# The recorder's reckoning of transfers set to longer landings, and one gate tile's room given to the common pool

## The chip, the cores and the metric

The kernel runs on one core of a Trainium2 chip. The metric is the device time of one execution in microseconds (us), lower being better. Three runs of the kernel before took 814.87, 815.20 and 815.69 us; the median is 815.20 us.

## The reference, cut to what matters

It computes one step of a one-layer decoder for 512 prompt tokens and 8 samples of 4 tokens, 544 columns in all, which share every weight:

```python
h = rmsnorm(x, norm_mix); z = h @ w_in             # attention and HGRN2 heads
x = x + concat([att, o]) @ w_out                   # 1024 wide
x = x + (cross-attention to 256 memory rows) @ w_co
u = rmsnorm(x, norm_ffn)
ug = u @ w_gate                                    # 1024 -> 2816
conv = conv_b + sum(conv_w[j] * up[:, j:j + T] for j in range(3))  # up: ug behind two kept rows
x = x + (silu(conv) * (u @ w_up)) @ w_down         # 2816 -> 1024
```

Everything is float32. The last two gate rows of each sequence are an output too.

## The kernel before, in words

Activations lie transposed, features on the 128 partitions and the 544 tokens along the row. Each float32 operand of a product is split in two rounded parts, a high one (h) and a low one (l): ScalarE (ACT) rounds the high part with a cast, VectorE (DVE) subtracts it to get the low one. A product is then three TensorE (PE) passes: high by high, high by low, low by high.

The feed-forward stage has 22 gate tiles g0 to g21 and 22 up tiles u0 to u21. The first six are computed plainly; the others in pairs by a scheme of seven half-size products in place of eight (class `Pair`, L2315). A pair's weights come in as one tile of 512 KB (wrg or wru, which holds A11 and A12), one of 256 KB (A22) and two sums S1 and S3. A sum is a 256 KB load on SyncE's queue (SP) followed by a second, adding transfer that GpSimd (POOL) issues into the same tile (`load_sum`, L2045). DVE makes S2 and S4 from S1. Each of the seven matrices is then split by a cast on ACT and a subtraction on DVE (`split_a`, L2076). On PE a pair's seven products run in the order 1, 2, 6, 7, 5, and its products 3 and 4 among those of the next pair. Products 1, 6, 5 and 3 add up in one bank of PE's memory, ps_a (ps_ag or ps_au by kind). Between them ACT copies that bank out: after product 1 into ps_d, after product 6 and after product 5 into a tile called kept (L2381). PE can't go on in that bank until the copy is done.

The down projection is three groups of such products on gate and up tiles 0 to 3, 4 to 7 and 8 to 11 (class `DownPair`, L2172), slipped between the pairs' products; a last part follows at the end. Its banks are ps_aw, ps_cw and ps_dw, and after its first product ACT copies ps_aw into ps_dw (L2241). A22 of two down pairs is loaded by POOL: two loads into A22w_h, a negating cast on ACT into A22w_l, and two adding loads into A22w_l (`load_split`, L2053). X, U, T and V (wX, wU and so on) are sums of tokens that DVE makes and ACT casts.

What sets the order of the work is a recorder, class `Tape`. The kernel's code doesn't issue instructions; it records steps, with the tiles that each reads and writes. PE's products of the main line keep a given order. `Tape.order` (L462) then plays all engines on a table of durations and so writes out one order per engine: at each moment an engine starts that step among the ready ones which is due first. A step may start when its due time is near (`lead`) and when its tiles' pools have room. The due times go backward from the main products (`due`, L417): a step is due its user's due time less `takes` (L263). For a transfer, `takes` and the moment at which its users become ready come from `Step.alone` (L269) and from the lines at L575 to L579: so many us fixed, so many for the bytes, alone and behind other transfers.

Each engine executes its instructions in the order so written and stops at one whose operand isn't there. SP and POOL issue transfers in that way too: an instruction whose tile is not yet free, or whose first load hasn't landed, holds up all behind it.

Two pools matter here. `A` (L736) gives tiles of 544 columns from a common pool of NA of them; weights, sums and parts come from it. `G` (feed-forward stage) gives tiles of 564 columns from a pool of NG: each gate tile ug and each convolution result cv takes one. A ug tile is free when the convolution has read it and POOL has copied its last rows into `last2` (L1991), a cv tile when the up tile has been multiplied by it.

Of the kernel before, what the change touches and what calls it, by code (L numbers as in the profile page):

```python
# [53 lines left out]

HT = N // 2
NBB = 12
NG = 5
LEVELS = (1, 2, 4, 8, 16, 32, 64)
FW = N
NA = 70  # L60


ROWS = [16 * i + j for i in range(96) for j in range(TS)] + list(range(1536, 2048))
# [189 lines left out]
class Step:  # L253
# [15 lines left out]
    def alone(self):  # L269

        if self.engine == "POOL":
            return 3.6 + 1.5 * self.bytes / 300e3 + 0.9 * (len(self.calls) - 1)
        return max(2.5 + self.bytes / 300e3, 1.1 + self.bytes / 170e3)


class Tape:
# [185 lines left out]
    def order(self):  # L462
# [22 lines left out]
        now, clock, bus, todo, done, burst, first = 0.0, [0.0, 0.0], 0.0, len(self.steps), [], False, None  # L485
# [15 lines left out]
        def held_back(s, after=0):  # L501

            block, wait = (codes + s.codes + len(hears(s)) // 2 + after - 1) // self.BLOCK, 0.0
            for b in range((codes - 1) // self.BLOCK + 1, block + 1):
                share = min(1.0, (b * self.BLOCK - codes) / s.codes)
                asked = now + max(0.0, ((b - 1) * self.BLOCK - 64 - codes) / s.codes) * s.length
                at = now + wait + share * s.length
                wait += max(0.0, fetched.get(b, asked + self.FETCH + queued()) - at)
            return wait
# [4 lines left out]
        def fetch(s, wait):  # L514
            nonlocal codes
            news = hears(s)
            codes += len(news) // 2
            heard.update(news)
            for b in range((codes - 1) // self.BLOCK + 1, (codes + s.codes - 1) // self.BLOCK + 1):
                fetched.setdefault(b + 1, now + wait + self.FETCH)  # L520
            for b in range((codes + 63) // self.BLOCK + 1, (codes + s.codes + 63) // self.BLOCK + 1):
                share = max(0.0, (b * self.BLOCK - codes - 64) / s.codes)
                fetched[b + 1] = now + share * (wait + s.length) + self.FETCH + queued()
            codes += s.codes
# [3 lines left out]
        def active(at):  # L528

            done = 0.0  # L530
            for a, b, work in reversed(ran):
                if b <= at - self.SPELL:
                    break
                done += work * (b - max(a, at - self.SPELL)) / (b - a)
            return done

        def needs(s):
            want = {}
            for n in s.tiles:
                if n in self.kinds and n not in held:  # L540
                    want[self.kinds[n]] = want.get(self.kinds[n], 0) + 1
            return want
# [22 lines left out]
        def start(s):  # L565
            nonlocal todo, bus, mode
            waiting[s.engine].remove(s)
            for k, v in needs(s).items():
                room[k] -= v
            for n in s.tiles:  # L570
                if n in last and n not in held:
                    ends[n] = last[n]
            held.update(n for n in s.tiles if n in self.kinds)
            s.start, s.nth = now, len(done)
            if s.bytes:  # L575
                pool = s.engine == "POOL"
                free[s.engine] = now + (0.9 * len(s.calls) if pool else 0.4)
                bus = max(bus, now) + (1.5 if pool else 1.0) * s.bytes / 300e3
                s.end = max(bus + (3.6 if pool else 2.5), now + s.alone())  # L579
            else:  # L580
                held_up = max(0.0, port[s.engine == "DVE"] - now) if s.port else 0.0
                if s.port:
                    port[s.engine == "POOL"] = now + held_up + s.length
                if s.engine == "PE":
                    held_up = held_back(s) + self.SWITCH * (s.mode != mode)
                    fetch(s, held_up)
                    mode = s.left_in
                    if now > 12.0 and now > cold[1] and active(now) < self.IDLE * self.SPELL:
                        cold[:] = cold[0] + self.COLD, now + 2 * self.SPELL
                    ran.append((now, now + held_up + s.length, s.work))  # L590
                free[s.engine] = s.end = now + held_up + s.length
            if s.main:
                clock[:] = s.est, now
            for n in s.tiles:
                if n in self.kinds:
                    left[n] -= 1
                    if not left[n]:
                        ends.pop(n, None)
                        frees.append((s.end + s.lag, self.kinds[n]))
            todo -= 1  # L600
            done.append(s)
            seen = set()
            for u in s.users:
                if u in seen:
                    continue
                seen.add(u)
                if s not in u.deps:
                    at = s.start
                elif u.engine == s.engine and not s.bytes:
                    at = s.start + s.length - 0.05  # L610
                else:
                    at = s.end + s.lag
                u.ready = max(u.ready, at)
                u.waits -= 1
                if not u.waits:
                    waiting[u.engine].append(u)

        while todo:
# [4 lines left out]
            for e in ("SP", "ACT", "DVE", "POOL"):  # L623
                if free[e] <= now + 1e-9:
                    at = clock[0] + min(now - clock[1], 4.0)
                    can = [s for s in waiting[e] if s.ready <= now + 1e-9 and s.begin <= at + (s.lead or self.LEAD) and fits(s)]
                    if can:
                        busy = port[e == "DVE"] > now + 0.1
                        start(min(can, key=lambda s: (s.begin + 2.0 * (s.port and busy), s.number)))
                        moved = True  # L630
            if free["PE"] <= now + 1e-9:
                can = [s for s in waiting["PE"] if s.ready <= now + 1e-9 and fits(s)]
                main = [s for s in can if s.main]
                side = [s for s in can if not s.main]
                if main:
                    side = [s for s in side if held_back(s, 96) < 0.1
                            and active(now + s.length) + s.work >= self.ACTIVE * self.SPELL]
                if side and first is None:
                    first = now
                even = [s for s in side if s.mode == s.left_in == mode == (128, 128)]  # L640
                if side and (burst or even or not main or sum(s.length for s in side) >= self.BURST
                             or now - first > self.PATIENCE
                             or min(s.begin for s in side) < clock[0] + now - clock[1]):
                    s = min(side, key=lambda s: (s.begin + self.NEAR * (s.mode != mode), s.number))
                    if not burst and even and main and sum(s.length for s in side) < self.BURST:
                        s = min(even, key=lambda s: (s.begin, s.number))
                    else:
                        burst, first = True, None
                    start(s)
                    moved = True  # L650
                elif main:
                    start(main[0])
                    burst = False
                    moved = True
            if not moved:
# [9 lines left out]
                now = min(t for t in later if t > now + 1e-9)  # L665
# [57 lines left out]
def tile_decoder_step(ctx: ExitStack, tc: tile.TileContext, xT, memT, kwT, vw, s0, conv_in, mkT, mv, vecs, cst,  # L723
# [12 lines left out]
    def A(name, shape=None, dt=F32):  # L736
        return tape.tile(act, shape or [128, FW], dt, tag="a", name=name, bufs=NA)

    def R(name):
        return tape.tile(act, [128, FW], F32R, tag="a", name=name, bufs=NA)[:, :N]  # L740

# [1199 lines left out]
    def G(name):  # L1941
        return tape.tile(ffn, [128, 564], F32, tag="g", name=name, bufs=NG)

# [847 lines left out]
```

## Time and profile before

| what | value |
| --- | --- |
| median of three runs | 815.20 us |
| the profiled execution's own time | 816.82 us |
| its span, first to last instruction | 815.0 us |
| PE busy | 795.2 us (98%) |
| DVE busy | 663.2 us (81%) |
| ACT busy | 465.7 us (57%) |
| POOL busy | 196.4 us (24%) |
| feed-forward stage | about 435 us to the end |
| granted TensorE clock | 0.997 |

The profile is one execution. Times in it are us from the span's start; the profiled run took 816.82 us, 1.8 us more than its span and 1.6 us more than the median. A row of the timeline is start, duration, engine, line, operation, output<-inputs, shapes and count, and in brackets how long the engine had been idle before it and what ended that. Buffer numbers are left out of its names: ps_dw is any down pair's ps_dw, and S3g6h is the high part of gate pair 6's S3. L718 and L690 are the lines of the recorder's wrapper, so all instructions have one of these two. SPq and POOLq rows are issues of transfers; a transfer's landing time is counted from its issue.

### The profile page before, as it was taken

To read this page: it belongs to the slowest core of one execution; us is meant where nothing else is said; L and a number is where in the kernel's file an instruction comes from. 1 tells how busy PE (TensorE), PEld (TensorE's weight loads), DVE (VectorE), ACT (ScalarE), POOL (GpSimd) and SP (SyncE) were. 2 spreads that over 40 slices of the span, in tenths; PEclk is the share of its full clock that TensorE was granted. 3 is DMA by queue.
4 is the path that set the end of the run, shared out by engine and by line. 5 is a ranking of instruction groups with operands and counts; after the bars stand their busy time and mean duration, and the time that the engine had idled before them with its cause. 6 is when DMAs were issued, how large, how long until landed. Compare 5 with 4: busy or idle time off the path is not lost.

```text
span 815.0 us, 19168 instructions
## 1 busy us (share of the span) xinstructions
PE 795.2 (98%) x7432; PEld 747.8 (92%) x7432; DVE 663.2 (81%) x1484; ACT 465.7 (57%) x996; POOL 196.4 (24%) x282
## 2 busy tenths in 40 slices
PE   9999999999999999999999998999899899999995
PEld 8998888987888889999899998999899899999995
DVE  6889786688598976654679898998999899989973
ACT  8724468616458454434466566655655666568642
POOL 1131100030120300312334144433334234141023
PEclk9999999999999999999999999999999999999998
DMA  9745996799742374362642386778678878876403
GB/s 316 238 144 148 316 288 187 261 331 304 232 140 82 108 253 136 101 191 90 183 139 58 74 209 148 170 161 209 158 170 162 194 170 173 197 185 196 102 2 110
DMA packets 106699, 143.35 MB, mean 176 GB/s; under 512 B 7280, under 2 KB 73712, under 8 KB 106608
## 3 DMA queue, kind: packets, MB, share of 16 engines
q1 hardware_dynamic: 91296, 123.77, 48.5%
q0 software_dynamic: 14592, 17.83, 14.2%
q8 instruction: 58, 0.95, 0.5%
q10 hardware_dynamic: 720, 0.53, 0.2%
q14 instruction: 33, 0.27, 0.1%
HBM read 134.04 MB, written 8.07 MB: 174 GB/s over the span
## 4 chain that ended last, share of the span: by engine, by line
PE 85%; DMA 6%; ACT 3%; DVE 3%; issue 1%; POOL 0%; SPq 0%; DVEq 0%; POOLq 0%; ACTq 0%
PE ps_wo L718 6%; PE ps_ag L718 4%; PE ps_au L718 4%; DMA S3g<-in_w_gate 4%; PE ps_aw L718 3%; PE ps_q L718 3%; PE ps_co L718 3%; PE ps_cq L718 3%; PE ps_dz L718 3%; PE ps_g L718 3%; PE ps_az L718 2%; PE ps_hv L718 2%; PE ps_first L718 2%; PE ps_cu L718 2%; PE ps_cg L718 2%; PE ps_ck L718 2%
## 5 line engine op out<-in xcount | busy, mean ns | idle before, releaser
L718 DVE TENSOR_TENSOR wl<-wr,wh 128x512 fp32r<-128x512 f32 x102 | 72.0, 729 | 1.2 <-ACT wh L718 1.2
L718 ACT CAST wh<-wr 128x512 fp32r<-128x512 f32 x102 | 58.5, 615 | 19.9 <-DMA wr<-in_w_out 7.0
L718 POOL TENSOR_TENSOR hG<-hG,hf 128x256 f32<-128x256 f32 (+1 forms) x28 | 25.0, 892 | 147.7 <-DVE hf L718 79.4
L718 POOL COPY last<-ug 128x2 f32<-128x2 f32 (+1 forms) x44 | 25.3, 618 | 94.1 <-DVE ug L718 84.0
L718 DVE SCALAR_TENSOR_TENSOR cv<-ug,vec,cv 128x560 f32<-128x560 f32 x44 | 35.1, 798 | 1.6 <-ACT cv L718 1.1
L718 POOL TENSOR_TENSOR acc_cx<-acc_cx,sq_cx 128x256 f32<-128x256 f32 (+1 forms) x14 | 11.5, 818 | 65.2 <-ACT sq_cx L718 65.2
L718 ACT ACTIVATE cv<-cv 128x560 f32<-128x560 f32 x22 | 14.8, 674 | 15.2 <-DVE cv L718 15.1
L718 ACT ACTIVATE cv<-ug,vec 128x560 f32<-128x560 f32 x22 | 18.8, 856 | 6.6 <-DVE ug L718 4.2
L718 POOL COPY ug<-conv_state 128x16 f32<-128x16 f32 x22 | 20.7, 941 | 0.0
L718 ACT ACTIVATE P<-P,mx 128x128 f32<-128x128 f32 (+3 forms) x32 | 17.6, 553 | 5.0 <-DVE mx L718 4.8
L718 DVE TENSOR_TENSOR xr<-xr,ps_wo 128x256 f32<-128x256 f32 (+1 forms) x16 | 6.9, 437 | 16.0 <-PE ps_wo L718 16.0
L690 POOL DMA_DIRECT2D S13w<-in_w_down x12 | 12.5, 1038 | 28.5 <-DVE cv L718 14.8
L718 PE MATMUL ps_co<-coh,wh 128*128 128x256 f32 (+1 forms) x64 | 19.2, 301 | 0.0
L718 PE MATMUL ps_co<-coh,wl 128*128 128x256 f32 (+1 forms) x64 | 18.4, 288 | 0.0
L718 PE MATMUL ps_co<-col,wh 128*128 128x256 f32 (+1 forms) x64 | 18.4, 287 | 0.0
L718 DVE TENSOR_TENSOR up<-ps_cu,keptu 128x272 f32<-128x272 f32 x20 | 8.7, 436 | 10.4 <-ACT keptu L718 8.0
L690 POOL DMA_DIRECT2D A22w_0l<-in_w_down x6 | 10.2, 1695 | 27.5 <-ACT S2g14h L718 10.5
L718 POOL TENSOR_TENSOR acc_ux<-acc_ux,sq_ux 128x256 f32<-128x256 f32 (+1 forms) x13 | 11.9, 916 | 17.7 <-ACT sq_ux L718 17.5
L718 POOL TENSOR_TENSOR acc_final<-acc_final,sq_final 128x256 f32<-128x256 f32 (+1 forms) x10 | 9.1, 922 | 28.4 <-ACT sq_final L718 28.4
L718 ACT COPY hsm<-psA 64x128 f32<-64x128 f32 x4 | 1.0, 259 | 26.1 <-PE psA L718 26.1
L718 DVE TENSOR_TENSOR xr<-xr,ps_aw 128x272 f32<-128x272 f32 x36 | 15.5, 430 | 0.3 <-PE ps_aw L718 0.3
L718 PE MATMUL psd<-st,qbd_win 128*32 128x224 f32 x256 | 15.6, 358 | 0.0
(3269 smaller groups left out, 3759.4 us busy)
## 6 DMA issues: line engine op xcount, KB each, us to landing
st<-in_kwT SPq DMA_DIRECT2D x32, 448.0 KB, 5.9
st<-in_vw SPq DMA_DIRECT2D x28, 512.0 KB, 6.4
wr<-in_w_in SPq DMA_DIRECT2D x25, 512.0 KB, 6.5
wru<-in_w_up SPq DMA_DIRECT2D x10, 512.0 KB, 6.9
wrg<-in_w_gate SPq DMA_DIRECT2D x9, 512.0 KB, 6.9
st<-in_mkT SPq DMA_DIRECT2D x8, 512.0 KB, 4.9
wr<-in_w_out SPq DMA_DIRECT2D x8, 512.0 KB, 4.7
S13w<-in_w_down SPq DMA_DIRECT2D x24, 128.0 KB, 3.1
```

What stands on the lines that cost most here:

```text
L690: return tape.put(engine, lambda: call(*args, **kw), outs, ins, 0.1, 0.3, size)
L718: return tape.put(engine, lambda: call(*args, **kw), outs, ins, length, lag, size, port, codes, work, mode)
```

## The change

Four lines of the recorder's table of transfers are other numbers, and two pool sizes:

```diff
-NG = 5
+NG = 4
-NA = 70
+NA = 71
...
         if self.engine == "POOL":
-            return 3.6 + 1.5 * self.bytes / 300e3 + 0.9 * (len(self.calls) - 1)
-        return max(2.5 + self.bytes / 300e3, 1.1 + self.bytes / 170e3)
+            return 5.5 + 2.0 * self.bytes / 300e3 + 0.9 * (len(self.calls) - 1)
+        return max(3.0 + self.bytes / 300e3, 1.1 + self.bytes / 90e3)
...
-                bus = max(bus, now) + (1.5 if pool else 1.0) * s.bytes / 300e3
-                s.end = max(bus + (3.6 if pool else 2.5), now + s.alone())
+                bus = max(bus, now) + (2.0 if pool else 1.0) * s.bytes / 300e3
+                s.end = max(bus + (5.5 if pool else 3.0), now + s.alone())
```

By this table a lone 256 KB transfer (262,144 bytes) of SP counted 3.4 us and now counts 4.0; one of 512 KB counted 4.2 and now 6.9; a 256 KB transfer of POOL counted 4.9 and now 7.2. No instruction of the computation is added or removed. The order in which ACT, DVE, POOL and SP have their instructions changes throughout the feed-forward stage and at many places before it. On PE the order of the main products is the same; between 95 us and 430 us the smaller products of attention, HGRN2 and cross attention stand at other places among them, and in the feed-forward stage PE's order is unchanged.

Three places, each before and after. The first is on POOL's queue, at the first down group (about 488 to 500 us of the profile). S1g6 and S3g6 are the adding transfers of gate pair 6, last2<-ug the copies of a gate tile's last rows, A22w0_0h the down group's loads. Before:

```order
L690 DMA S1g6_1464<-in_w_gate 128x512
L718 COPY last2_1250<-ug5_1413 128x2
L718 COPY last2_1250<-ug5_1413 128x16
L690 DMA S3g6_1471<-in_w_gate 128x512
L718 COPY last2_1250<-ug4_1390 128x2
L718 COPY last2_1250<-ug4_1390 128x16
L690 DMA A22w0_0h_1496<-in_w_down 128x2x128 x2
```

After:

```order
L690 DMA S1g6_1464<-in_w_gate 128x512
L690 DMA A22w0_0h_1496<-in_w_down 128x2x128
L690 DMA S3g6_1471<-in_w_gate 128x512
L690 DMA A22w0_0h_1496<-in_w_down 128x2x128
L718 COPY last2_1250<-ug5_1413 128x16
L718 COPY last2_1250<-ug5_1413 128x2
L718 COPY last2_1250<-ug4_1390 128x2
L718 COPY last2_1250<-ug4_1390 128x16
```

S3g6's transfer stood behind the copies of ug5 and now stands ahead of them, with one load of A22w0_0h ahead of it. At the second and third groups (S3g10, S3g14) the copies already stood ahead of the transfers; there both loads of A22w_0h, which stood behind S3g's transfer, now stand between S1g's and S3g's, with copies of a gate tile between the two loads.

The second place is ACT's queue at the second down group (about 567 to 575 us): casts, a convolution's start (cv9), the copy of ps_au8 into kept that PE's product 3 waits for, and the copy of ps_aw0 into ps_dw. Before, directly behind the cast of S1g10:

```order
L718 ACTIVATE cv9_1616<-ug9_1577,vec_72 128x560
L718 CAST S3g10h_1650<-S3g10_1649 128x512
L718 CAST A22u8h_1655<-A22u8_1654 128x512
L718 COPY keptu8_1605<-ps_au8_1583 128x272
L718 CAST wXh4_1487<-wX4_1481 128x272 x2
L718 CAST S24w4_0h_1640<-S24w4_0_1639 128x512
L718 CAST wUh4_1485<-wU4_1482 128x272
L718 ACTIVATE A22w4_0l_1675<-A22w4_0h_1674 128x512
L718 COPY ps_dg10_1624<-ps_ag10_1623 128x272
L718 CAST wUh4_1485<-wU4_1482 128x272
L718 CAST S2g10h_1644<-S2g10_1643 128x512
L718 COPY ps_dw0_1629<-ps_aw0_1628 128x272
```

After, from that cast on:

```order
L718 CAST S1g10h_1671<-S1g10_1642 128x512
L718 CAST A22u8h_1655<-A22u8_1654 128x512
L718 ACTIVATE A22w4_0l_1675<-A22w4_0h_1674 128x512
L718 ACTIVATE cv9_1616<-ug9_1577,vec_72 128x560
L718 COPY keptu8_1605<-ps_au8_1583 128x272
L718 CAST S24w4_0h_1640<-S24w4_0_1639 128x512
L718 CAST wUh4_1485<-wU4_1482 128x272 x2
L718 CAST S3g10h_1650<-S3g10_1649 128x512
L718 COPY ps_dg10_1624<-ps_ag10_1623 128x272
L718 CAST S2g10h_1644<-S2g10_1643 128x512
L718 COPY ps_dw0_1629<-ps_aw0_1628 128x272
```

The cast of S3g10 moved from ahead of the copy into kept to behind it. The cast of A22u8 and the negating cast A22w4_0l now both stand ahead of cv9, and the casts of wX stand behind the copy into ps_dw. At the third group (632 to 641 us) it is alike, but there the casts of wX stay ahead of the copy into ps_dw and the cast of S3g14 stands ahead of them. At the first group (502 to 509 us) the casts of A22u4, S1g6 and h4 come ahead of S3g6's, and behind it stand wX, A22w0_0l, S24w0_0, wX and the first half of wU, and only then the copy into kept; behind that, the second half of wU, cv5, S2g6, ps_dg, A11u6, and then the copy into ps_dw.

The third place is ACT's queue at about 714 us, where up pair 18 begins; ps_du18 is the copy that PE's product 2 waits for. Before:

```order
L718 CAST S4u18h_2030<-S4u18_2029 128x512
L718 CAST h17h_1991<-up17_1965 128x544
L718 COPY ps_du18_2000<-ps_au18_1999 128x272
L718 COPY ug18_1978<-ps_ag18_1969 128x240
L718 COPY ug18_1978<-ps_ag18_1969 128x8x4
L718 ACTIVATE cv18_2004<-ug18_1978,vec_72 128x560
```

After:

```order
L718 CAST S4u18h_2030<-S4u18_2029 128x512
L718 COPY ps_du18_2000<-ps_au18_1999 128x272
L718 CAST S1g20h_2051<-S1g20_2037 128x512
L718 COPY ug18_1978<-ps_ag18_1969 128x240
L718 COPY ug18_1978<-ps_ag18_1969 128x8x4
L718 ACTIVATE cv18_2004<-ug18_1978,vec_72 128x560
L718 CAST S2g20h_2039<-S2g20_2038 128x512
L718 CAST h17h_1991<-up17_1965 128x544
```

The cast of h17 moved from ahead of that copy to behind it, and one of S1g20 stands there instead.

At the last of ACT's places of which the prediction speaks (735 to 745 us, up pair 20) the casts of S4u20 and A22u20 change sides about the copy into ps_du20, and a cast into wdh and one into A11h change sides about the first copy into kept; the number of casts ahead of the second copy is the same.

On SP, in the mixing stage, some loads of weights (wr) moved behind one or more loads of cached rows (st), as wr16 behind st35; in the feed-forward stage S1g10's load moved ahead of A1w4_0's and S1g14's ahead of A1w8_0's.

## Prediction

> **What bounds the kernel now.** First the page's busy times, then the busy times by stretches of the feed-forward stage (columns: PE, weight load, DVE, ACT, POOL, clock, DMA share, GB/s).
>
> ```profile
> PE 795.2 (98%) x7432; PEld 747.8 (92%) x7432; DVE 663.2 (81%) x1484; ACT 465.7 (57%) x996; POOL 196.4 (24%) x282
> 450.00:500.00 50.00, 50.00 (x400) 50.00 (x399) 45.90 (x91) 29.48 (x56) 17.47 (x25) 1.00 0.58 144
> 50.00:310.00 260.00, 259.51 (x3034) 223.50 (x3027) 212.18 (x562) 143.20 (x322) 33.29 (x41) 1.00 0.68 213
> 571.40:637.50 66.10, 63.71 (x504) 63.27 (x504) 60.48 (x130) 39.92 (x84) 23.23 (x36) 1.00 0.79 176
> 637.50:703.00 65.50, 63.81 (x503) 63.25 (x504) 62.48 (x130) 41.58 (x86) 22.31 (x37) 1.00 0.76 171
> ```
>
> PE bounds it, at full clock. Where it never stops it issues 400 products in 50 us, 0.125 us each; 12 of them, one half-size product of a pair, take 1.5 us. What it can still gain is its stops, listed by the waits and shown one by one by the timeline:
>
> ```profile
> PE ps_dw L718 <- ACT ps_dw L718: 4.2, 3, 1.7
> PE ps_au L718 <- ACT keptu L718: 3.7, 4, 1.4
> 506.09 0.40 PE L718 MATMUL ps_au<-B22h,S4u4h 128*128 128x272 f32 x1 [1.36 <-ACT keptu L718]
> 508.68 0.39 PE L718 MATMUL ps_dw<-h1h,A1w_0h 128*128 128x272 f32 x1 [0.82 <-ACT ps_dw L718]
> 571.44 0.40 PE L718 MATMUL ps_au<-B22h,S4u8h 128*128 128x272 f32 x1 [0.60 <-ACT keptu L718]
> 574.88 0.39 PE L718 MATMUL ps_dw<-h5h,A1w_0h 128*128 128x272 f32 x1 [1.67 <-ACT ps_dw L718]
> 637.51 0.39 PE L718 MATMUL ps_au<-B22h,S4u12h 128*128 128x272 f32 x1 [0.69 <-ACT keptu L718]
> 640.96 0.39 PE L718 MATMUL ps_dw<-h9h,A1w_0h 128*128 128x272 f32 x1 [1.67 <-ACT ps_dw L718]
> 715.13 0.39 PE L718 MATMUL ps_du<-B21h,A12u18h 128*128 128x272 f32 x1 [0.50 <-ACT ps_du L718]
> 745.02 0.39 PE L718 MATMUL ps_au<-B22h,S4u20h 128*128 128x272 f32 x1 [1.04 <-ACT keptu L718]
> ```
>
> Eight stops, 8.35 us; the first product behind a stop runs 0.1 us longer (0.40 against 0.29), so they cost 9.2 us. Why ACT copies so late is in its timeline, and for the first stop in POOL's:
>
> ```profile
> 502.71 0.62 ACT L718 CAST S3g6h<-S3g 128x512 fp32r<-128x512 f32 x1 [2.42 <-DMA S3g<-in_w_gate]
> 503.24 0.42 ACT L718 CAST h4h<-up 128x272 fp32r<-128x272 f32 x1
> 503.56 0.62 ACT L718 CAST A22u4h<-A22u 128x512 fp32r<-128x512 f32 x1
> 504.92 0.85 ACT L718 ACTIVATE cv<-ug,vec 128x560 f32<-128x560 f32 x1
> 505.67 0.36 ACT L718 COPY keptu<-ps_au 128x272 f32<-128x272 f32 x1
> 567.26 0.62 ACT L718 CAST S1g10h<-S1g 128x512 fp32r<-128x512 f32 x1 [2.82 <-DMA S1g<-in_w_gate]
> 569.96 0.62 ACT L718 CAST S3g10h<-S3g 128x512 fp32r<-128x512 f32 x1 [1.32 <-DMA S3g<-in_w_gate]
> 571.01 0.38 ACT L718 COPY keptu<-ps_au 128x272 f32<-128x272 f32 x1
> 632.50 0.62 ACT L718 CAST S1g14h<-S1g 128x512 fp32r<-128x512 f32 x1 [2.35 <-DMA S1g<-in_w_gate]
> 635.29 0.62 ACT L718 CAST S3g14h<-S3g 128x512 fp32r<-128x512 f32 x1 [2.18 <-DMA S3g<-in_w_gate]
> 637.10 0.36 ACT L718 COPY keptu<-ps_au 128x272 f32<-128x272 f32 x1
> 493.77 3.81 POOL L718 COPY last<-ug 128x2 f32<-128x2 f32 x2 [4.83 <-DVE ug L718]
> 497.53 0.86 POOL L690 DMA_DIRECT2D S3g<-in_w_gate  x1
> ```
>
> ACT stands still for a sum that hasn't landed, with the copy that PE needs queued behind the cast. The old table put those casts too early: it counted 4.9 us for POOL's adding transfer, and the table of issues has more (KB each, median us to landing):
>
> ```profile
> S1g<-in_w_gate POOLq DMA_DIRECT2D x9, 256.0 KB, 6.1
> S3g<-in_w_gate POOLq DMA_DIRECT2D x9, 256.0 KB, 7.0
> S3g<-in_w_gate SPq DMA_DIRECT2D x9, 256.0 KB, 3.3
> A22w_0h<-in_w_down POOLq DMA_DIRECT2D x6, 128.0 KB, 8.4
> ```
>
> The Trainium skill ("DMA: Bandwidth & Descriptors", on the anatomy of a DMA issued by GpSimd) gives about 2.0 us plus the bytes at 436 GB/s. By that page a 256 KB transfer would take an estimated 2.6 us, the old table would already be generous, and the change would gain nothing. The rows disagree here: 7.0 us in the median, with a second transfer ahead on the same queue and a DMA share near 0.8.
>
> **The change part by part.** ACT steps follow each other at 0.32 us (a cast of 272, 503.24 to 503.56), 0.53 (a cast of 512, 502.71 to 503.24), 0.75 (cv, 504.92 to 505.67), about 0.3 (a copy).
>
> *First group.* S3g6's transfer no longer stands behind ug5's copies, which held it until 497.53. Its base was long there, so it goes behind S1g6's and one load, some 6 us sooner, and lands before ACT comes to it: the 2.42 us stand-still goes. Next late is DVE: one wU cast now stands ahead of the copy into kept.
>
> ```profile
> 502.83 0.78 DVE L718 TENSOR_TENSOR wU<-wX,up 128x272 f32<-128x272 f32 x2
> ```
>
> The first wU is ready near 503.3, so the copy runs near 503.7, in time for PE, which came to it at 504.73 (506.09 less 1.36): 1.36 saved. Behind the copy stand wU, cv5, S2g6, ps_dg and A11u6, 0.3 + 0.32 + 0.75 + 0.53 + 0.3 + 0.53 = 2.7 us, so the copy into ps_dw starts near 506.4. PE goes on 0.43 us behind a copy's start (505.67 to 506.09), at 506.8; it is there at 504.73 + 1.5 = 506.2 and waits 0.6 in place of 0.82. Saved: 1.5.
>
> *Second group.* S3g10's cast stands behind the copy into kept, but the negating cast of A22w now stands ahead of it. If that finds its data, the copy comes at 567.26 + 0.53 + 0.53 + 0.53 + 0.75 = 569.6, before PE needs it at 570.84, and ps_dw's copy, 2.8 us behind it, lets PE go on at 572.8, against its 572.3: 0.5 of 0.60 + 1.67 is left, 1.8 saved. If A22w0h lands only where S3g10 landed (569.96, now being ahead of it on POOL's queue), the copy comes at 571.2, and 0.8 and 1.3 are left: near nothing saved. If it lands 8.4 us after an issue at 562.7, at 571.1, the copy comes at 572.4, and 1.1 is lost.
>
> ```profile
> 562.00 1.54 POOL L690 DMA_DIRECT2D A22w_0h<-in_w_down  x2
> ```
>
> I take 1.3, nearer the upper end: the two small loads are ahead of S3g's transfer now, so they no longer wait for its bytes, and S1g10's base load moved ahead of another on SP.
>
> *Third group.* Likewise: found in place, the copy comes at 634.9 in place of 637.10 and ps_dw's, 3.4 us behind it as before, lets PE go on at 638.7, against its 638.3: 2.0 saved. If A22w0h lands at 635.29, as S3g14 did, the copy is where it was: nothing saved. Two us later it loses 2.0. I take 1.0. DVE allows no more: 62.48 us of its work stand in those 65.50.
>
> *Up pair 18.* The cast of h17 leaves the place ahead of ps_du's copy:
>
> ```profile
> 714.15 0.65 ACT L718 CAST h17h<-up 128x544 fp32r<-128x544 f32 x1
> 714.70 0.38 ACT L718 COPY ps_du<-ps_au 128x272 f32<-128x272 f32 x1
> ```
>
> The copy comes 0.55 sooner and the wait of 0.50 goes. *Up pair 20*: as many casts as before stand ahead of its copy, so 1.04 stays.
>
> *Before 430 us.* PE loses 0.49 us of 260 there, so little can be gained; smaller products shift by a main product or two. Bound: 0.5 gained to 1.5 lost (three stops like that one); I take 0. Weights' loads behind cached rows' cost nothing:
>
> ```profile
> 149.59 0.37 SPq L690 DMA_DIRECT2D st<-in_vw  x1
> 168.11 3.05 PE ps_hq L718 x24
> wr<-in_w_in SPq DMA_DIRECT2D x25, 512.0 KB, 6.5
> ```
>
> wr16, now behind the 149.59 load, lands near 156.5, 11.6 us ahead of its first product; without that cover each us late would be a us of PE.
>
> *The pools.* One more common tile lets a load go one release sooner: nothing by itself. Four gate tiles hold what a pair needs at once (two ug, two cv); cost 0 while the tile comes free in time, bounded by the fourth rival.
>
> Sum: 1.5 + 1.3 + 1.0 + 0.5 = 4.3, and 0.1 for each of some four stops that vanish, 4.7. The profiled run's 816.82 becomes 812.1; against the median of 815.20, 1.6 lower, it is **810.5 us**.
>
> **The rivals.** *All stops go* (0.12): shorter stand-stills let the copies follow each product at once; 815.2 - 9.2 = 806.0. Against it: the work on ACT between the two copies is longer than PE's 1.5 us.
>
> *The stand-stills only change their names* (0.15): A22w0h lands late in both groups (-1.1, -2.0), which eats the 1.5 and 0.5 saved elsewhere: 816.3; milder, some 814 to 815. The landing of 8.4 us speaks for it, its place ahead of S3g against it.
>
> *The longer reckoning moves casts for nothing* (0.03): transfers are short, 815.2. Only the page above speaks for it.
>
> *Slower: the fourth gate tile* (0.15). cv of a new pair now waits until DVE has multiplied an earlier up tile; ACT stands, and the copies behind it with it. A wait of ACT for DVE in this stage looks so:
>
> ```profile
> ACT cv L718 <- DVE cv L718: 10.4, 12, 2.1
> ```
>
> 0.87 us in the mean; passed on to PE in each of nine gate pairs it is 7.8: 815.2 - 4.7 + 7.8 = 818.3. It decides from 0.52 us per pair. DVE's 92 to 95% busy speaks for it; against it, an earlier up tile is done well before.
>
> **How the numbers follow.** The forecast has 0.55, its own range 808 to 813.5. A measurement can tell 0.2%, 1.6 us. Faster: 0.55 + 0.12 + 0.03 of the renamed stand-stills = 0.70. Same: 0.08 of these and 0.03 = 0.11. Slower: the gate tile and 0.04 = 0.19. The range, 805.5 to 816.5, takes in the forecast, both of the unknown landings' ends and all stops gone; outside lie the gate tile and the worst of the renamed stand-stills, 0.19 in all.
>
> **What would show it.** Right: no ACT idle for S3g6 near 502, S3g6 issued near 490, the PE waits for kept and ps_dw down from 7.9 to about 4, that at up pair 20 still there. Wrong: ACT idle ahead of A22w_0l or cv, named DMA or DVE; PE idle between 95 and 430 us above 2 us; DVE idle as before with PE waiting for it.

## The result, and the profile after

The changed kernel takes 807.71 us (median of four runs, 807.61 to 808.49), the kernel before 815.05 us (four runs, 814.87 to 815.69): a ratio of 0.9911, with a 95% interval of 0.9894 to 0.9928. It is faster by 7.3 us, where 4.7 us was forecast. The profiled execution took 808.49 us with a span of 806.7, against 816.82 and 815.0 before.

The busy times of the page, after:

```profile
PE 793.3 (98%) x7432; PEld 745.7 (92%) x7432; DVE 664.9 (82%) x1484; ACT 466.8 (58%) x996; POOL 200.2 (25%) x282
```

PE was busy 795.2 us before: 1.9 of the 8.3 us by which the span is shorter; the rest it had stood still. Where it stood shows in the stretches of the feed-forward stage, after (columns: PE, weight load, DVE, ACT, POOL, clock, DMA share, GB/s). The second and third rows cover the work of the second and third groups, as the two 66 us rows shown of before do.

```profile
435.00:506.00 71.00, 71.00 (x563) 70.79 (x563) 66.70 (x138) 45.73 (x87) 25.32 (x42) 1.00 0.52 124
566.90:633.00 66.10, 66.10 (x530) 66.10 (x529) 63.38 (x136) 43.16 (x92) 27.34 (x39) 1.00 0.83 185
633.00:698.50 65.50, 65.50 (x524) 65.50 (x524) 62.40 (x128) 41.37 (x85) 24.46 (x36) 1.00 0.78 182
```

PE has no gap left in any of the three; before, it lost 2.39 and 1.69 us in the later two and issued 504 and 503 products where it now issues 530 and 524. DVE has as much work as before in the third stretch (62.40 us against 62.48), and PE doesn't stop for it.

The waits of PE in the whole span, after (us in total, times, longest):

```profile
PE ps_au L718 <- ACT keptu L718: 1.1, 1, 1.1
PE psr_mem L718 <- DVE acc_mem L718: 0.5, 1, 0.5
PE psr_mix L718 <- DVE acc_mix L718: 0.5, 1, 0.5
PE psL L718 <- ACT hsm L718: 0.2, 1, 0.2
```

The ps_dw wait of 4.2 us is gone, that for kept is down from 3.7 to 1.1. The one left is at up pair 20. The timeline of PE and ACT at the places of the eight stops, after:

```profile
501.61 0.62 ACT L718 CAST S3g6h<-S3g 128x512 fp32r<-128x512 f32 x1
504.29 0.38 ACT L718 COPY keptu<-ps_au 128x272 f32<-128x272 f32 x1
506.99 0.38 ACT L718 COPY ps_dw<-ps_aw 128x272 f32<-128x272 f32 x1
562.47 0.62 ACT L718 CAST S1g10h<-S1g 128x512 fp32r<-128x512 f32 x1
564.47 0.63 ACT L718 ACTIVATE A22w_0l<-A22w_0h 128x512 fp32r<-128x512 f32 x1
566.34 0.39 ACT L718 COPY keptu<-ps_au 128x272 f32<-128x272 f32 x1 [0.48 <-PE ps_au L718]
567.78 0.62 ACT L718 CAST S3g10h<-S3g 128x512 fp32r<-128x512 f32 x1
569.38 0.39 ACT L718 COPY ps_dw<-ps_aw 128x272 f32<-128x272 f32 x1
570.63 0.29 PE L718 MATMUL ps_dw<-h5h,A1w_0h 128*128 128x272 f32 x1
629.51 0.39 ACT L718 COPY keptu<-ps_au 128x272 f32<-128x272 f32 x1 [0.48 <-PE ps_au L718]
632.95 0.39 ACT L718 COPY ps_dw<-ps_aw 128x272 f32<-128x272 f32 x1
705.58 0.37 ACT L718 COPY ps_du<-ps_au 128x272 f32<-128x272 f32 x1
736.61 0.39 PE L718 MATMUL ps_au<-B22h,S4u20h 128*128 128x272 f32 x1 [1.05 <-ACT keptu L718]
```

No cast in these rows carries a wait for a DMA any more. At the second and third groups the brackets have turned round: the copy into kept now waits for PE (0.48 us), not PE for it. POOL's queue at the first group, and the transfers of the sums as the table of issues has them (KB each, median us to landing), both after:

```profile
487.00 1.11 POOL L690 DMA_DIRECT2D S1g<-in_w_gate  x1
488.33 1.42 POOL L690 DMA_DIRECT2D S3g<-in_w_gate  x1
494.52 3.38 POOL L718 COPY last<-ug 128x16 f32<-128x16 f32 x4 [4.02 <-DVE ug L718]
```

```profile
S1g<-in_w_gate POOLq DMA_DIRECT2D x9, 256.0 KB, 4.0
S3g<-in_w_gate POOLq DMA_DIRECT2D x9, 256.0 KB, 5.0
A22w_0h<-in_w_down POOLq DMA_DIRECT2D x6, 128.0 KB, 4.8
```

S3g6's transfer is issued at 488.33, ahead of the copies, where it was at 497.53 behind them. The four copies take 3.38 us here, as two took 3.81 before; no sum of this group waits behind them any more. And the landings have become shorter in this execution: 4.0, 5.0 and 4.8 us where they were 6.1, 7.0 and 8.4. Why isn't shown, and the gain doesn't need it: f4_ffn_new below, with a stage as short, has 6.2, 6.0 and 7.2.

From PE's first gate product (ps_g, at 435.54 us before and 436.94 after) to the end of its last product (806.56 and 798.21) the profiled executions show 371.02 and 361.27 us: 9.75 us less. Ahead of that product 1.40 us was lost. From one first product of a pair to another the stage gained 2.64 us at the first group (g6 to u6), 2.81 at the second (g10 to u10), 3.36 at the third (g14 to g18) and 0.74 at up pair 18 (g18 to u20).

### The profile page after: what moved, and what is told of

The parts are those of the page before. It is cut to its first block, busy times and chain, and to the rows that moved or that the text cites. A ratio compares the mean times of both kernels' runs of the same rounds, so it can differ in the third digit from the quotient of the medians.

```text
span 806.7 us, 19149 instructions
## 1 busy us (share of the span) xinstructions
PE 793.3 (98%) x7432; PEld 745.7 (92%) x7432; DVE 664.9 (82%) x1484; ACT 466.8 (58%) x996; POOL 200.2 (25%) x282
## 4 chain that ended last, share of the span: by engine, by line
PE 89%; DVE 4%; ACT 3%; DMA 1%; issue 1%; SPq 0%; DVEq 0%; ACTq 0%
PE ps_au L718 7%; PE ps_ag L718 7%; PE ps_wo L718 6%; PE ps_aw L718 4%; PE ps_cu L718 4%; PE ps_cg L718 3%; PE ps_co L718 3%; PE ps_q L718 3%; PE ps_g L718 3%; PE ps_cq L718 3%; PE ps_dz L718 3%; PE ps_az L718 3%; PE ps_cw L718 2%; PE ps_hv L718 2%; PE ps_cv L718 2%; PE ps_du L718 2%
## 5 line engine op out<-in xcount | busy, mean ns | idle before, releaser
L718 DVE TENSOR_TENSOR wl<-wr,wh 128x512 fp32r<-128x512 f32 x102 | 74.2, 749 | 0.5 <-ACT wh L718 0.5
L718 ACT CAST wh<-wr 128x512 fp32r<-128x512 f32 x102 | 58.4, 618 | 12.3 <-DMA wr<-in_w_in 8.1
L718 POOL COPY last<-ug 128x16 f32<-128x16 f32 (+1 forms) x44 | 32.5, 776 | 56.1 <-DVE ug L718 51.9
L718 ACT ACTIVATE P<-P,mx 128x128 f32<-128x128 f32 (+3 forms) x32 | 17.6, 555 | 2.5 <-DVE mx L718 2.5
L718 POOL COPY ug<-conv_state 128x16 f32<-128x16 f32 x22 | 18.5, 875 | 0.0
L718 ACT COPY keptg<-ps_ag 128x272 f32<-128x272 f32 x18 | 6.9, 386 | 18.4 <-PE ps_ag L718 18.4
L718 ACT ACTIVATE cp<-ps_cp,cmx 128x256 f32<-128x256 f32 x16 | 7.5, 472 | 15.2 <-DVE cmx L718 15.2
L718 POOL TENSOR_TENSOR acc_ux<-acc_ux,sq_ux 128x256 f32<-128x256 f32 (+1 forms) x13 | 11.6, 891 | 17.8 <-ACT sq_ux L718 17.6
L718 POOL TENSOR_SCALAR cp<-cp,cden 128x256 f32<-128x256 f32 x8 | 8.2, 1024 | 30.4 <-DVE cden L718 24.0
```

The lines of the kernel that those rows point to most:

```text
L718: return tape.put(engine, lambda: call(*args, **kw), outs, ins, length, lag, size, port, codes, work, mode)
```

## The experiments

The theory: PE's stops are late copies of ACT, and the copies are late because a cast that waits for a transfer stands ahead of them; the longer landings put that right by placing the casts later and issuing the transfers sooner. The first rival: the pool sizes do it, not the numbers. Ratios below are to the kernel before in the same job, a set of runs taken together; its medians there were 814.46 us (812.65 to 817.69) for e1 to e4, 812.95 (809.56 to 816.75) for f1 to f4 and 811.56 (809.77 to 815.85) for g1 to g3. "Stage" is the time from the first gate product to PE's last, as above, in one profiled execution, which need not be a typical one: f2's took 818.26 us where its median is 815.60.

| kernel | us | ratio, 95% interval | stage, us |
| --- | --- | --- | --- |
| before | see above | 1 | 371.02 |
| changed | 807.71 | 0.9911 (0.9894 to 0.9928) | 361.27 |
| e1_sizes | 808.86 | 0.9922 (0.9897 to 0.9947) | 364.00 |
| e2_numbers | 807.21 | 0.9901 (0.9864 to 0.9937) | 360.88 |
| e3_due_only | 807.95 | 0.9911 (0.9879 to 0.9943) | 362.10 |
| e4_landing_only | 807.58 | 0.9904 (0.9873 to 0.9935) | 361.83 |
| f1_casts_behind | 812.57 | 0.9997 (0.9981 to 1.0013) | 368.24 |
| f2_loads_ahead | 815.60 | 1.0037 (1.0020 to 1.0054) | 370.71 |
| f3_ng4 | 812.05 | 0.9993 (0.9973 to 1.0012) | 365.94 |
| f4_ffn_new | 805.94 | 0.9922 (0.9893 to 0.9951) | 360.84 |
| g1_room_only | 809.72 | 0.9974 (0.9957 to 0.9990) | 364.88 |
| g2_less_room | 808.76 | 0.9958 (0.9943 to 0.9973) | 361.52 |
| g2b_less_room69 | 827.45 | 1.0177 (1.0150 to 1.0205) | 372.81 |
| g3_short | 852.03 | 1.0457 (1.0395 to 1.0520) | 400.01 |

### The parts of the change

**e1_sizes**: the sizes alone, with the old table.

```diff
-NG = 5
+NG = 4
-NA = 70
+NA = 71
```

> The two pool sizes alone (4 gate tiles, 71 common tiles) with the old table of transfers. Theory L (the longer landings do it): ACT still stands for sums in the feed-forward stage, within 2 us of the kernel before, 813 to 817. Theory R (room does it: the extra common tile lets loads go earlier): near the changed kernel, 807 to 809. If four gate tiles cost anything, it shows here: above 817.

Measured: 808.86 us. **e2_numbers**: the new table alone, with NG 5 and NA 70.

> The new table of transfers alone, with the old pool sizes (5 gate tiles, 70 common tiles). Theory L: near the changed kernel, 807 to 810, PE's waits for kept and ps_dw below 2 us. Theory R: near the kernel before, 814 to 816.

Measured: 807.21 us. **e3_due_only**: sizes as changed, the new numbers only in `takes`, from which the due times come; the landings that the recorder plays are the old ones.

```diff
-        return self.lag + self.alone()
+        return self.lag + self.alone_due()
...
```

> New pool sizes; the longer times count only in the due times (when a transfer ought to start), while the recorder still plays the landings with the old numbers. Theory A (the gain is that transfers are issued sooner): most of the gain, 807 to 810, gate pair 10's S1 transfer on POOL issued 13 us or more ahead of its first product. Theory B (the gain is that casts stand later on ACT, behind the copies): little of it, 812 to 816, that transfer issued about 8 us ahead as before.

Measured: 807.95 us. **e4_landing_only**: the other half; new numbers in the landings played, old ones in the due times.

> New pool sizes; the longer times count only in the landings that the recorder plays, while due times keep the old numbers. Theory A: little of the gain, 812 to 816, with ACT standing for sums. Theory B: most of it, 807 to 810, though gate pair 10's S1 transfer is issued only some 8 us ahead of its first product.

Measured: 807.58 us. All four give the gain of the whole, within the intervals: the sizes without the table (e1), the table without the sizes (e2). So the parts don't add up; they are several ways out of one bad order. For the same reason e3 and e4, which both have the new sizes, can't decide between due times and landings, though each took the time that its own theory named. S1g10's adding transfer goes 15.2 us ahead of its pair's first product in e3 and 10.8 in e4, where it was 8.1 before. e1 still has casts that wait for DMA and a stop for ps_dw; e2 has no such stop and one such cast. From e1's waits of PE:

```profile
PE ps_dw L718 <- ACT ps_dw L718: 1.4, 1, 1.4
```

The theory that the numbers are needed falls; what the old order had that all the others lack was still open.

### The mechanism by hand, in the old order

**f1_casts_behind**: the kernel before, with five casts moved on ACT's queue and nothing else; at the second group, for instance:

```diff
-CAST S1g10h
 ACTIVATE cv9
-CAST S3g10h
 CAST A22u8h
 COPY keptu8
+CAST S1g10h
+CAST S3g10h
```

> The kernel before, old table, old sizes, every queue as it was but ACT's: five casts (S3g6, S1g10, S3g10, S1g14, S3g14) stand directly behind the copy into kept that they stood ahead of. Theory (a copy is late because a cast that waits for its transfer stands ahead of it): the three kept stops at these places (1.36, 0.60, 0.69) go, and of the ps_dw stops (0.82, 1.67, 1.67) about 1.5 is left, since the casts now stand ahead of those copies; 2.65 + 2.66 and 0.1 for each stop that goes make 5.7: 809.5 us. Rival (the plan as a whole, its loads above all, makes the difference): nothing moves but names, 814 us or more.

**f2_loads_ahead**: the kernel before, with only transfers moved; on SP, at the second group (likewise at the third; on POOL, S3g6 ahead of the copies of ug5):

```diff
+DMA S1g10
+DMA S3g10
 DMA S13w4_0 x2
 DMA A1w4_0
-DMA S1g10
-DMA S3g10
```

> The kernel before, ACT's, DVE's and PE's queues unchanged; only the transfers go sooner: S3g6's adding transfer ahead of two copies on POOL, the loads of S1g10, S3g10, S1g14 and S3g14 ahead of S13w's and A1w's on SP. Theory (it is the landing that counts, not the place of the cast): S3g6 lands some 5 us sooner, the other sums some 2, ACT's idle times of 2.42, 2.82, 1.32, 2.35 and 2.18 fall to under 1 each and the six stops of 6.8 us to about 1: 809 us. Rival (the sums are the first of several late operands, or the loads that were pushed back come late in their place): 814 us or more, with ACT idle ahead of S13w or A1w instead.

**f3_ng4**: the kernel before with one gate tile fewer.

```diff
-NG = 5
+NG = 4
```

> The kernel before with NG 4 for 5 and nothing else; the order of instructions on every engine is the same. Theory (a cv tile comes free in time): no change, 815 us within 0.8, no new wait of ACT at cv. Rival (the fourth gate tile holds cv up until an earlier up tile has been multiplied): 0.87 us for each of nine gate pairs, up to 818 to 822 us.

f1 and f2 missed: 812.57 us, no gain, and 815.60 us, slower by 0.37%. f3 came out as the theory had it, no change. But f3's profile is also a second execution of the old order, word for word, and it shows that the other two were reckoned from stops that this order doesn't always have. POOL's copies at the first group and PE's stop at the second, in f3:

```profile
493.31 1.29 POOL L718 COPY last<-ug 128x2 f32<-128x2 f32 x2 [5.15 <-DVE ug L718]
494.54 0.85 POOL L690 DMA_DIRECT2D S3g<-in_w_gate  x1
572.56 0.40 PE L718 MATMUL ps_dw<-h5h,A1w_0h 128*128 128x272 f32 x1 [1.61 <-ACT ps_dw L718]
```

The copies that took 3.81 us in the profile before took 1.29 us here, S3g6's transfer left 3 us sooner, and neither stop of the first group is there, nor are the stops for kept of the second and third. The profile before was one of the bad executions of an order whose stops come and go: over all jobs the kernel before ran 53 times, from 809.56 to 817.69 us. That the new order is steadier shows in the job of g1 to g3, where the kernel before's 18 runs cover 6.1 us and g2's nine, in the changed kernel's order, 1.5. (The changed kernel's own four lie within 0.9 us, but so do the kernel before's four in that job.) The changed kernel ran in its first job alone, and there the kernel before had the highest median of the four jobs, 815.05 against 814.46, 812.95 and 811.56 us: the 7.3 us are that job's.

In f1 the stops for kept are gone too, though f3 shows that they can go without the edit, and the casts now stand ahead of the copy into ps_dw. ACT and PE at the second group, then PE's products in the 4 us behind that stop (columns as above), in f1:

```profile
567.69 0.62 ACT L718 CAST S3g10h<-S3g 128x512 fp32r<-128x512 f32 x1 [1.06 <-DMA S3g<-in_w_gate]
571.38 0.38 ACT L718 COPY ps_dw<-ps_aw 128x272 f32<-128x272 f32 x1
571.81 0.40 PE L718 MATMUL ps_dw<-h5h,A1w_0h 128*128 128x272 f32 x1 [1.91 <-ACT ps_dw L718]
```

```profile
571.80:576.00 4.20, 4.19 (x21) 4.19 (x22) 3.09 (x8) 2.40 (x6) 4.20 (x7) 0.59 0.81 119
```

S3g10 still lands where it landed; the wait has gone from the copy into kept to the next copy, and the stop there is longer than f3's 1.61. The clock behind it was granted at 0.59 for 4.2 us, which by that share cost another 4.2 x 0.41 = 1.7 us. In f2 the base load of S1g10 goes 14.9 us ahead of its pair in place of 12.0, but its second transfer only 8.9 in place of 8.1. POOL's queue in f2:

```profile
559.00 0.90 POOL L690 DMA_DIRECT2D S13w<-in_w_down  x1 [1.50 <-DMA S13w<-in_w_down]
559.57 1.22 POOL L690 DMA_DIRECT2D S1g<-in_w_gate  x1
567.34 0.62 ACT L718 CAST S1g10h<-S1g 128x512 fp32r<-128x512 f32 x1 [2.66 <-DMA S1g<-in_w_gate]
```

S13w's transfer stands ahead of it and now waits for the load that was pushed back; ACT waits 2.66 us for S1g10, about as before (2.82). That is the rival written for f2, the one that loads pushed back come late in their place. So neither of the two moves by hand paid. In the changed kernel the loads of the group go sooner together. S1g10's load and adding transfer, before and then after:

```profile
556.44 0.34 SPq L690 DMA_DIRECT2D S1g<-in_w_gate  x1
560.32 0.85 POOL L690 DMA_DIRECT2D S1g<-in_w_gate  x1 [1.76 <-DMA S1g<-in_w_gate]
```

```profile
548.22 0.41 SPq L690 DMA_DIRECT2D S1g<-in_w_gate  x1
553.18 1.22 POOL L690 DMA_DIRECT2D S1g<-in_w_gate  x1
```

Counted to the first product of gate pair 10 (568.43 before, 566.89 after) the load's lead is 18.7 us where it was 12.0, that of the adding transfer 13.7 where it was 8.1. That all loads must go sooner isn't shown. In e4 S3g10's adding transfer goes 7.9 us ahead, hardly more than the 7.5 of before, and yet its cast, which stands behind the copy into kept and ahead of that into ps_dw, finds it landed (in e4 the wrapper's lines are L724 and L696):

```profile
556.97 0.86 POOL L696 DMA_DIRECT2D S3g<-in_w_gate  x1 [1.39 <-DMA S3g<-in_w_gate]
566.30 0.62 ACT L724 CAST S3g10h<-S3g 128x512 fp32r<-128x512 f32 x1
```

PE has no stop for kept or ps_dw at any of e4's three groups. Whether the sooner loads or the later casts do it stays open.

**f4_ffn_new**: the changed kernel, with the new numbers only for transfers recorded from the feed-forward stage on, where `Step.SLOW` turns true.

```diff
+        self.slow = Step.SLOW
...
+        if self.engine == "POOL" and not self.slow:
+            return 3.6 + 1.5 * self.bytes / 300e3 + 0.9 * (len(self.calls) - 1)
...
```

> The changed kernel (NG 4, NA 71), but the new table counts only for transfers that are recorded from the feed-forward stage on; those before count by the old. Theory (the new table gains in the feed-forward stage and loses 1.4 us before it): both gains together, 806.3 us, its first gate product back near 435.5 us. Rival (the earlier part is not the table's but that of the tile and of chance in the plan): 807.7 us or more.

Measured: 805.94 us, close to the 806.3 expected, with its first gate product at 434.88 us and without the waits psr_mem and psL. But its ratio of 0.9922 is no better than the changed kernel's 0.9911; it ran in another job, and in that job the kernel before was quicker too. That it beats the changed kernel isn't shown.

### Order or room

The old order with room for one tile more, and the new order with one and two fewer. In all three the recorder plans with the number that it had; only the pool differs (in the diff for g1, with NG 4 and NA 71).

```diff
-            self.rooms[kw["tag"]] = kw["bufs"]
+            self.rooms[kw["tag"]] = 70 if kw["tag"] == "a" else kw["bufs"]
```

**g1_room_only**:

> The kernel before with its own order on every engine, word for word (the recorder still plans with 70 common tiles), but 71 tiles are there and 4 gate tiles. Theory (SP stands at its queue until a tile comes free, so the loads of the sums go late whatever their place): each load goes one release sooner, S1g10's base load more than 14 us ahead of its pair where it was 12.0, the stops for kept and ps_dw fall to about 2 us: 809.5 us. Rival (the tile helps only a plan that counts on it): as the kernel before, within 1 us.

Measured: 809.72 us, 0.26% less than before. The time is the theory's, but not its reason: S1g10's base load goes 12.3 us ahead of its pair's first product (565.93), not over 14. SP in g1 at the second group:

```profile
553.60 0.36 SPq L690 DMA_DIRECT2D S1g<-in_w_gate  x1
```

ACT still waits for S3g10 there and ps_dw still stops PE for 1.7 us. The interval of g1 overlaps that of f3 (0.9973 to 1.0012), the same order with 70 tiles, so what the tile adds to that order isn't clear of the noise.

**g2_less_room** (the changed kernel's order, NA 70):

> The changed kernel with its own order on every engine (planned with 71 common tiles), but only 70 are there. Theory (room sets the transfers' lead): the loads go one release later, S1g10's base load some 14 to 16 us ahead of its pair where it was 18.7, and a ps_dw stop or two is back: 809 us. Rival (the order alone, casts behind copies and loads in another order, holds the gain): 807.7 us, no stop but the one of up pair 20.

Measured: 808.76 us, 0.42% less than before, the stage 361.52 us, as in the changed kernel with its 361.27. SP and ACT in g2:

```profile
549.77 0.45 SPq L690 DMA_DIRECT2D S1g<-in_w_gate  x1
566.82 0.63 ACT L718 ACTIVATE A22w_0l<-A22w_0h 128x512 fp32r<-128x512 f32 x1 [0.75 <-DMA A22w_0h<-in_w_down]
```

The time is near the theory's 809, but the profile is the rival's. With the tile taken away again S1g10's load still goes 18.6 us ahead, and in the whole stage only this one instruction of ACT waits for a transfer. What the profile has over the changed kernel's lies ahead of the stage (first gate product at 438.31, 436.94 there). So the lead comes from the order and not from the tile that is there; it is 17.6 us in e2, planned by the new table with 70 tiles, and 14.9 in e1, planned by the old one with 71.

**g2b_less_room69** (the same order, NA 69):

> The changed kernel with its own order, but only 69 common tiles: two releases later. Theory (room): leads of 12 us or less, as in the kernel before, stops of 4 us or more: 812 us or more. Rival (the order alone): 808 us.

Measured: 827.45 us, in the theory's direction (812 us or more), but not for its reason: S1g10's load still goes 18.3 us ahead, not 12. Room does bound the time, but as a cliff: one tile less than planned costs the stage 0.25 us, two cost 11.5, and 7.5 more are lost ahead of it (first gate product at 444.43). Nor are these 11.5 the stops of the old order: no instruction of ACT waits for a DMA in this stage. PE stops for other engines, here at up pair 2, and the clock behind the stop drops; what the missing tiles hold up first isn't shown. PE, and the 4.7 us from there, in g2b:

```profile
490.34 0.39 PE L718 MATMUL ps_au<-Th,S1u2h 128*128 128x272 f32 x1 [1.94 <-ACT keptu L718]
```

```profile
490.30:495.00 4.70, 4.66 (x25) 4.66 (x26) 4.70 (x9) 2.20 (x4) 0.00 (x0) 0.64 0.99 280
```

### Shorter landings

**g3_short**: sizes as changed, and a table with short landings (the diff is to the old table).

```diff
-            return 3.6 + 1.5 * self.bytes / 300e3 + 0.9 * (len(self.calls) - 1)
+            return 2.0 + self.bytes / 436e3 + 0.9 * (len(self.calls) - 1)
-        return max(2.5 + self.bytes / 300e3, 1.1 + self.bytes / 170e3)
+        return 2.0 + self.bytes / 436e3
...
-                bus = max(bus, now) + (1.5 if pool else 1.0) * s.bytes / 300e3
-                s.end = max(bus + (3.6 if pool else 2.5), now + s.alone())
+                bus = max(bus, now) + s.bytes / 436e3
+                s.end = max(bus + 2.0, now + s.alone())
```

> Sizes as changed (NG 4, NA 71), but a table with short landings: 2.0 us and the bytes at 436 GB/s for every transfer, 2.6 us for 256 KB. Theory (the reckoning decides how far ahead a transfer goes and where its cast stands): transfers go later and casts stand sooner than by the old table, ACT idles for DMA longer than with the old table and 71 tiles, several stops are back: 813 us or more. Rival (only the tile and the chance of a new plan count): 808 to 809 us, as with the old table and 71 tiles.

Measured: 852.03 us, a ratio of 1.0457. Its longest waits of PE, and one sum on its way through SP, POOL, ACT and PE:

```profile
PE ps_au L718 <- ACT keptu L718: 9.3, 6, 2.5
PE ps_dw L718 <- ACT ps_dw L718: 7.0, 7, 1.4
PE ps_ag L718 <- ACT keptg L718: 6.9, 4, 2.7
```

```profile
568.82 0.34 SPq L690 DMA_DIRECT2D S3g<-in_w_gate  x1
574.62 0.86 POOL L690 DMA_DIRECT2D S3g<-in_w_gate  x1 [2.96 <-DMA S3g<-in_w_gate]
581.38 0.62 ACT L718 CAST S3g10h<-S3g 128x512 fp32r<-128x512 f32 x1 [4.98 <-DMA S3g<-in_w_gate]
584.75 0.40 PE L718 MATMUL ps_au<-B22h,S4u8h 128*128 128x272 f32 x1 [2.39 <-ACT keptu L718]
```

The load is issued at 568.82, its base has landed 5.8 us later, the sum another 6.8 us after that; ACT stands 4.98 us at the cast, and PE stops 2.39 us for the copy behind it. This is the mechanism of the theory at its plainest, and with the tile there: with the same sizes, the old table gives 0.9922 and this one 1.0457. Not all of it is stops: over the stage the granted clock is 0.97, and PE's first gate product comes at 441.76, 4.8 us later than in the changed kernel. The Trainium skill ("DMA: Bandwidth & Descriptors", on the anatomy of a DMA issued by GpSimd) has 2.0 us and the bytes at 436 GB/s, 2.6 us for these 256 KB by the estimate from it; the rows have 4.0 to 7.0. As what a lone transfer costs at best it may stand, no run here shows one; as the time that a planner may count on beside this stage's other transfers it fails.

## Why the prediction was right or wrong

- **What bounds it** held: PE, at full clock, less its stops. Seven of the eight stops went, and that at up pair 20 stayed, 1.04 us before and 1.05 after, as forecast. The waits for kept and ps_dw are down from 7.9 us to 1.1, where about 4 was expected.
- **What a stop costs** was mis-sized: its bracket and 0.1 us. A bracket counts only from the end of the product before, which runs 0.29 us, while PE otherwise starts the next after 0.125. The products before and behind that at 506.09, in the profile before:

```profile
504.44 0.29 PE L718 MATMUL ps_aw<-h0h,A1w_0l 128*128 128x272 f32 x1
506.32 0.29 PE L718 MATMUL ps_au<-B22l,S4u4h 128*128 128x272 f32 x1
```

  They start 1.88 us apart where two products take 0.25: 1.63 us lost, 0.27 more than the bracket of 1.36. With 0.27 for each, the seven stops that went make 7.31 + 1.89 = 9.2 of the stage's 9.75 us; all eight would have made 10.5 and not 9.2.
- **The first group** was mis-sized a little: 2.18 us of stops went, 1.5 was forecast. The copy into ps_dw came 2.70 us behind that into kept, as reckoned (504.29 and 506.99); but that into kept came 1.6 us before PE needed it (505.89), where the reckoning, which let wU hold it, had 1.0, so nothing is left of the 0.6 us.
- **The second and third groups** were the failing terms: 1.3 and 1.0 us forecast, stops of 2.27 and 2.36 gone. Two cautions failed. A22w's landing, taken between its 8.4 us and nothing, fell to 4.8 us in the median and held nothing up. And "DVE allows no more" was wrong: DVE has 62.40 us of work in those 65.50 us, and the stops are gone. The copy into ps_dw follows 3.04 and 3.44 us behind that into kept, near the 2.8 and 3.4 reckoned; what was missed is when ACT reaches the copy into kept. The reckoning starts from S1g10's cast at 567.26, behind its wait of 2.82 us, and so leaves that wait in; in the changed kernel this cast stands 4.4 us ahead of its pair's first product where it came 1.2 ahead, waits for nothing, and the copy into kept is done before PE needs it.
- **Up pair 18**: right, the stop of 0.50 went with the cast of h17 (ps_du's copy at 705.58).
- **Before 430 us** was taken at nothing, between 0.5 gained and 1.5 lost; the profiled execution lost 1.40. What of that is the change isn't settled: executions of the old order have their first gate product between 435.22 and 437.30 us. That the 4.7 us of the forecast and the 7.3 measured lie so near is in part luck: in the profiles the stage gained 9.75 us, twice the forecast, and the 1.40 lost ahead of it made up for some of that.
- **The pools**: one gate tile fewer costs nothing (f3: 0.9993), so that rival is out. "One more common tile: nothing by itself" was wrong by at most 1.8 us (g1), which is not clear of f3's noise; but a plan that counts on it is worth as much as the whole change (e1).
- **The rivals.** That all stops go (806.0) came nearest, nearer than the forecast itself; by the cost of a stop found above it should have said 804.7. The forecast's 810.5 was the old ACT queue with a few waits taken out, where the new order takes out their cause. The renamed stand-stills didn't come about in the changed kernel; f1 shows one, with S3g10's cast in place of A22w's. The rival that transfers are short and the change is for nothing is out: the medians of 4.0 to 7.0 us are long, and g3, planned with short ones, is the slowest of all.
- **The reason given** is right in the mechanism and too narrow in the cause. A late landing ahead of the copies is what stops PE (g3). But it was told as the old table's fault alone; e1 and e2 show that either the sizes or the table lead to an order with little or nothing of it. And the eight stops, read from one execution as if fixed, were those of one at 816.82 us, which only two of the 53 exceed.

What stays open: whether sooner loads or later casts are what the new order needs, why one execution of the old order has POOL's copies at 3.81 us and another at 1.29, what the 69 tiles of g2b hold up, and whether f4's earlier part is really better.

## What to carry to other kernels

When a planner's table is corrected, look at the order that comes of it, not at the table: how much lead each transfer gets over its first user (here 18.7 us in place of 12.0), and what stands behind a cast that may wait. Moving a few casts or loads by hand only handed the wait on to the next step. Reckon landings long rather than short: this longer table cost nothing that these runs could show, the short one cost 40 us. And before stops are added up from one profile, run the same order again: a stop behind a landing differs from execution to execution, and part of what a change seems to save may be that. Count a stop from start to start of the products about it, not by its idle time alone.

## What the runs showed of the hardware that was not expected

- **The time to landing is no constant of the transfer.** S3g's adding transfers of 256 KB have medians of 7.0 us before, 5.0 after; the loads of A22w_0h 8.4 and 4.8. Even in the same order they differ: A22w_0h has 8.4 in the profile before and 6.5 in f3's.
- **A stop of some 2 us can cost nearly that again in clock.** Behind 1.91 us in f1 the granted clock was 0.59 for 4.2 us, behind 1.94 us in g2b 0.64 for 4.7 us; behind the stops of 1.67 us before it stayed at 1.00, and so it did behind one of 1.90 us in f2 and one of 1.96 us in g2b (at 754.71). The windows behind the first and the second of these, the last column but two the clock, in before and in f2:

```profile
640.90:645.00 4.10, 4.04 (x32) 4.05 (x33) 4.10 (x12) 3.07 (x8) 4.10 (x7) 1.00 0.68 114
```

```profile
638.60:643.00 4.40, 2.73 (x19) 2.51 (x20) 4.28 (x10) 4.40 (x12) 1.24 (x2) 1.00 0.27 70
```

  So it happens in some places only (in the second row PE is idle for a second stop of 1.67 us, at an unchanged clock), and what decides isn't shown. The Trainium skill ("TensorE: Matmul & The Clock Gate", Part 1) has half clock after an idle window of about 3.4 us; here a shorter idle time was enough.
- **Two small copies on POOL (128x2 and 128x16)** took 3.81 us in one execution and 1.29 in another of the same order, and a transfer queued behind them left 3 us later. The long pair lasts from 493.77 to 497.58, and beside it five operations of DVE on 128x512 run back to back from 493.72 to 496.81. In f3 the same five begin at 493.26, and yet both copies are done by 494.60; what decides isn't shown.
